# A decoder trunk in split fp32: another order of gates, VectorE's y work spread out, and adding transfers ordered behind GpSimd's powers

## The chip, the cores and the metric

The kernel runs on one core of a Trainium2 chip. The metric is the device time of one execution in microseconds (us), as the median of several runs. TensorE (PE) multiplies, VectorE (DVE) and ScalarE (ACT) work on tiles, GpSimd (POOL) does a few small steps and issues transfers, SyncE (SP) issues most transfers.

## The reference

512 tokens of 1024 features pass one layer; 16 learned meta tokens stand ahead of them and are dropped at the end. All is fp32.

```python
h = concat([pad, meta, x])
h = h + 0.5 * swiglu(rms_norm(h, ffn1_norm), ffn1_w_in, ffn1_w_out)
h = h + token_mixer(rms_norm(h, mix_norm), ...)
h = h + 0.5 * swiglu(rms_norm(h, ffn2_norm), ffn2_w_in, ffn2_w_out)

# rms_norm(x, g) = x * rsqrt(mean(x * x) + EPS) * g
# swiglu(h, w_in, w_out): gate, up = split(h @ w_in); (silu(gate) * up) @ w_out   (2816 hidden units)
# token_mixer: proj = h @ w_in, split into q, k, v of both branches and ga, gb (1024 each)
#   o_fox = attention with a forget gate; o_swa = sliding-window attention with sinks
#   y = sigmoid(ga) * (o_fox @ w_branch_fox) + sigmoid(gb) * (o_swa @ w_branch_swa)
#   return y @ w_out
```

## The kernel before

**Products.** Every fp32 factor is split into a hi part and a lo part: ScalarE casts the hi part (L133), VectorE subtracts it from the value (L140, or L142 with a scale). A product is then three matmuls per 128 rows: weight hi by data hi (L293), weight hi by data lo (L294), weight lo by data hi (L296). In names, `wh`/`wl` are the parts of a weight piece, `xH`/`xL` of the normalised tokens, `yH`/`yL` of `y`, `oW`/`oLs` of an attention output.

**Sevens.** Most large products are done two weight blocks at a time with seven products instead of eight (`seven`, L504), over halves of the tokens and of the inner dimension. The weights of such a unit are loaded as pieces A to D: A is the first blocks and a sum, loaded plainly (SP's queue, `land`, L206) and with an accumulating transfer on GpSimd's queue (`add`, L210) that adds the second block in DRAM to what landed; B, C and D come from `rawC` (also with an add) and `rawD`; VectorE makes B's sums `tc` of both (L232, L233), just before they are cast to `wh` and subtracted to `wl`. The data side needs sums too: S1 to S4, each a pair of hi and lo parts. The first two units of each feed-forward are plain products (gate and up, both token halves).

**Stages**, by the names of the trace: entry, up to 31 us, where token blocks are loaded, their mean squares made, raised to the power -1/2 on GpSimd (`rsq`, L337), scaled (`entry_scale`, L641) and transposed by TensorE (`to_features`, L649); FFN1 to about 375; the mixer's projections and both attentions to about 608; the gates to 700; the output projection to 747; FFN2 to the end.

**The entry.** Blocks 0 to 2 (272 tokens with the meta tokens) go first, blocks 3 and 4 (256 tokens) in `enter_rest` and `enter_second`: one step on VectorE makes both mean squares into `rin`, GpSimd raises both, VectorE scales `xt3` and `xt4`, TensorE transposes each in eight steps.

**The gates.** The first four column blocks (NG = 4) of the fox gate are plain products. For the rest the table `GATES` (L41) gives the order of sevens: (b, m) is column blocks m and m + 1 of the gate of branch b (0 is fox, 1 is sliding). A fox gate multiplies `zA`, which holds the fox branch's output, by its sigmoids. A sliding gate with m below 6 multiplies `oA`, the sliding branch's output, by its sigmoids (`sg`), adds `zA` and makes `yH` and `yL` (`y_out`); with m = 6 it keeps its sigmoids for the two products marked "sliding", which finish `y` (`last_y`). The output projection then goes over two token halves `hf` with eight column blocks `mi` each, and reads all of `y` of its token half; `add_out` adds it to the residual `h2T` and sums squares. Its second half is followed by the power for FFN2 in two parts, r2 (`second_rms`).

**What sets the order.** The code states work in an order, and a scheduler puts each engine's instructions in a row by that order and by hints (`issue_after`, here `after`). Each engine then takes its row strictly in order and waits at semaphores. Loads are stated five pieces ahead of use (`load_to`); `holds` stops them at certain pieces until `release()` is called: after the second rms of the entry, after the attention's buffers are freed, and in FFN2 after the second power.

Of the kernel before, what the change touches and what calls it, by code (L numbers as in the profile page):

```python
# [11 lines left out]
F32 = mybir.dt.float32  # L12
# [8 lines left out]
P = 128  # L21
D = 1024
KD = D // P
S = 512
# [15 lines left out]

GATES = [(1, 0), (1, 2), (0, 4), (1, 4), (0, 6), (1, 6), ("sliding", 6), ("sliding", 7)]  # L41
TH = T // 2
# [40 lines left out]
def kernel(  # L83
# [46 lines left out]
    def hi(o, i, scale=None):  # L130

        if scale is None:
            return A.copy(o, i)  # L133
        return A.activation(o, i, AF.Identity, scale=scale)
# [74 lines left out]
    def add(tile_, ap):  # L209
        G.dma_start(tile_[:, : 128 * ap.shape[1]].rearrange("p (k c) -> p k c", c=128), ap, accum_op=ALU.add)  # L210

# [47 lines left out]
    def release():  # L259
        del holds[0]  # L260

    def split_to(n):
# [73 lines left out]
    def rsq(o, i):  # L336
        G.tensor_tensor(out=o, in0=i, in1=nhalf[: i.shape[0], : i.shape[1]], op=ALU.pow)  # L337

# [1224 lines left out]


    for k in range(0, KD, 4):
        A.dma_start(xg[:, k : k + 4], h1d[:, k : k + 4])
# [29 lines left out]
    xq = lambda tok, feat: xg[:, 4 * feat : 4 * feat + 4, halves[tok]]  # L1596

    at = [spare[:, 2 * i : 2 * i + 2].rearrange("p a (b c) -> p (a b) c", c=HF) for i in (0, 1, 2, 0)]

    def sum_of(i, a, b, op=ALU.subtract):  # L1600
        V.tensor_tensor(out=at[i], in0=a, in1=b, op=op)

    def parts_of(i, name):
        hi(xS[name][:, 0], at[i])
        lo(xS[name][:, 1], at[i], xS[name][:, 0])

    with after(*shared["split"]):
        sum_of(0, xq(0, 0), xq(1, 0))
    parts_of(0, "S3")
# [20 lines left out]
    def y_out(m, c, s):  # L1630
        tt(s, s, zA[:, m, c], ALU.add)
        hi(yH[:, m, c], s)
        lo(yL[:, m, c], s, yH[:, m, c])

    def last_y(m):
        def use(ps):
            s = swa_out(m)
            tt(s, s, ps)
            y_out(m, slice(0, S), s)

        return use
# [54 lines left out]
    h2T = kp.tile([P, KD, S], F32, tag="z", name="h2T")  # L1696
    x2 = kp.tile([P, KD, S], F32, tag="o", name="x2")
    for k in (slice(0, 2), slice(2, KD)):
# [26 lines left out]

    X2 = Halves(None, x2, S // 2)
    for hf in range(2):
        c = slice(S // 2 * hf, S // 2 * (hf + 1))
        for mi in range(KD):
            run(feat_steps(piece, yH, yL, KD, S // 2 * hf, add_out(mi, c), w=S // 2))  # L1730
            if hf and mi == 0:
# [143 lines left out]
```

## Time and profile before

| | us |
|---|---|
| median of 3 runs | 1092.93 (1091.42 to 1093.97) |
| profiled execution, its own time | 1091.91 |
| its span, first to last instruction | 1090.1 |
| PE busy, 8587 instructions | 1072.3 (98%) |
| DVE busy | 891.5 (82%) |
| ACT busy | 656.3 (60%) |
| POOL busy | 194.2 (18%) |

The granted clock of TensorE is 0.998 over the span. A row of the timeline gives the start in us, the duration, engine, line, operation, output and inputs, and in brackets how long the engine was idle before and what ended that. Instructions of one engine overlap: matmuls are pipelined, so a matmul of 0.28 us is followed by the next after about 0.12 us.

### The profile page before, as it was taken

The page shows a single profiled execution, that of the slowest core. Times are in us where ns is not written, and L with a number is a line of the kernel's source. Part 1 is how long each engine was busy: PE and PEld are TensorE (multiplying, and loading weights), DVE is VectorE, ACT ScalarE, POOL GpSimd, SP SyncE. Part 2 cuts the span into 40 slices and gives each one's busy share as a digit, 9 for nine tenths or more (in the row PEclk, how much of TensorE's full clock was granted, in tenths as well). Part 3 has the DMA queues.
Part 4 walks back from the last instruction along what each step waited for, and adds up shares of the span by engine and source line. Part 5 has one row for each costly group of instructions (what it writes and reads, how often), then busy time and mean ns, then how long its engine had stood idle before and what let it go on. Part 6 is the DMA issues. An engine that isn't in the chain of part 4 may idle for free.

```text
span 1090.1 us, 22316 instructions
## 1 busy us (share of the span) xinstructions
PE 1072.3 (98%) x8587; PEld 1038.8 (95%) x8587; DVE 891.5 (82%) x1712; ACT 656.3 (60%) x1241; POOL 194.2 (18%) x229
## 2 busy tenths in 40 slices
PE   7999999999999999999999999999999999999998
PEld 6999999999999999999987799999999999999998
DVE  5978878888889677778897699878998778887895
ACT  5676546646666455456667866545676466645664
POOL 2011111121114430222200110001122211221120
PEclk9999999999999999999999999999999999999999
DMA  8586777678776423112211764467588877886753
GB/s 287 146 221 170 174 193 199 160 197 231 169 191 162 129 77 120 58 60 60 80 59 59 229 166 128 143 224 212 143 207 176 203 189 178 182 195 182 168 119 105
DMA packets 111723, 173.06 MB, mean 159 GB/s; under 512 B 10800, under 2 KB 58160, under 8 KB 111232
## 3 DMA queue, kind: packets, MB, share of 16 engines
q1 hardware_dynamic: 74032, 122.03, 34.6%
q0 software_dynamic: 28768, 37.83, 21.8%
q10 hardware_dynamic: 8816, 11.77, 3.4%
q8 instruction: 67, 1.10, 0.4%
q14 instruction: 40, 0.33, 0.1%
HBM read 167.37 MB, written 6.32 MB: 159 GB/s over the span
## 4 chain that ended last, share of the span: by engine, by line
PE 56%; DVE 6%; ACT 2%; DMA 1%; issue 1%; POOL 0%; ACTq 0%; DVEq 0%; POOLq 0%
PE ps L293 9%; PE ps L296 8%; PE ps L294 8%; PE pt L293 8%; PE pt L294 8%; PE pt L296 8%; DVE wl L140 2%; ACT wh L133 1%; DMA rawC<-in_wg_dram 1%; ACT t L1159 1%; DVE oA L1629 1%; PE pt L1199 1%; PE pt L1244 1%; PE ps L1366 0%; DMA raw<-in_wout_dram 0%
## 5 line engine op out<-in xcount | busy, mean ns | idle before, releaser
L293 PE MATMUL ps<-x,wh 128*128 128x256 f32 (+2 forms) x768 | 219.6, 286 | 1.1 <-ACT pt L514 1.0
L294 PE MATMUL ps<-x,wh 128*128 128x256 f32 (+2 forms) x768 | 219.0, 285 | 0.5 <-DVE x L142 0.4
L296 PE MATMUL ps<-x,wl 128*128 128x256 f32 (+2 forms) x768 | 218.9, 285 | 0.0
L140 DVE TENSOR_TENSOR wl<-raw,wh 128x1024 fp32r<-128x1024 f32 (+3 forms) x125 | 150.2, 1202 | 46.8 <-ACT wh L133 45.2
L133 ACT CAST wh<-raw 128x1024 fp32r<-128x1024 f32 (+3 forms) x125 | 128.4, 1029 | 90.2 <-PE ps L294 56.6
L293 PEld LDWEIGHTS ps<-x,wh 128*128 128x128 f32 x768 | 144.7, 189 | 2.6 <-ACT pt L514 1.2
L294 PEld LDWEIGHTS ps<-x,wh 128*128 128x128 f32 x768 | 144.5, 188 | 1.5 <-DVE x L142 0.9
L296 PEld LDWEIGHTS ps<-x,wl 128*128 128x128 f32 x768 | 144.6, 188 | 0.9
L293 PE MATMUL pt<-x,wh 128*128 128x256 f32 (+2 forms) x424 | 125.4, 296 | 0.2 <-ACT wh L133 0.2
L296 PE MATMUL pt<-x,wl 128*128 128x256 f32 (+2 forms) x424 | 124.5, 294 | 0.0
L294 PE MATMUL pt<-x,wh 128*128 128x256 f32 (+2 forms) x392 | 112.6, 287 | 0.0
L140 DVE TENSOR_TENSOR wl<-tc,wh 128x1024 fp32r<-128x1024 f32 (+1 forms) x70 | 83.5, 1193 | 32.9 <-ACT wh L133 32.6
L133 ACT CAST wh<-tc 128x1024 fp32r<-128x1024 f32 (+1 forms) x70 | 71.8, 1026 | 59.2 <-DVE tc L233 51.3
L293 PE MATMUL ps<-acts,wh 128*128 128x264 f32 (+1 forms) x352 | 100.5, 285 | 0.3 <-ACT pt L514 0.2
L296 PE MATMUL ps<-acts,wl 128*128 128x264 f32 (+1 forms) x352 | 99.8, 284 | 0.0
L294 PE MATMUL ps<-acts,wh 128*128 128x264 f32 (+1 forms) x352 | 99.5, 283 | 0.0
L140 DVE TENSOR_TENSOR wl<-rawC,wh 128x1024 fp32r<-128x1024 f32 (+1 forms) x70 | 84.1, 1202 | 6.1 <-ACT wh L133 5.8
L133 ACT CAST wh<-rawC 128x1024 fp32r<-128x1024 f32 (+1 forms) x70 | 71.6, 1023 | 22.5 <-PE pt L294 16.1
L293 PEld LDWEIGHTS pt<-x,wh 128*128 128x128 f32 x424 | 80.0, 189 | 2.6 <-ACT wh L133 0.4
L296 PEld LDWEIGHTS pt<-x,wl 128*128 128x128 f32 x424 | 79.7, 188 | 2.1
L294 PEld LDWEIGHTS pt<-x,wh 128*128 128x128 f32 x392 | 73.7, 188 | 0.6
L293 PEld LDWEIGHTS ps<-acts,wh 128*128 128x128 f32 x352 | 66.5, 189 | 0.9 <-ACT pt L514 0.4
(417 smaller groups left out, 3249.7 us busy)
## 6 DMA issues: line engine op xcount, KB each, us to landing
rawC<-in_w1i_dram SPq DMA_DIRECT2D x20, 512.0 KB, 4.3
raw<-in_w1i_dram SPq DMA_DIRECT2D x40, 256.0 KB, 4.0
raw<-in_w2i_dram SPq DMA_DIRECT2D x40, 256.0 KB, 3.5
rawC<-in_w2i_dram SPq DMA_DIRECT2D x20, 512.0 KB, 4.4
raw<-in_wm_dram SPq DMA_DIRECT2D x18, 512.0 KB, 4.3
raw<-in_wout_dram SPq DMA_DIRECT2D x16, 512.0 KB, 4.1
rawD<-in_w1i_dram SPq DMA_DIRECT2D x20, 256.0 KB, 4.2
rawC<-in_w1i_dram POOLq DMA_DIRECT2D x20, 256.0 KB, 5.8
```

The lines of the kernel that those rows point to most:

```text
L133: return A.copy(o, i)
L140: return V.tensor_tensor(out=o, in0=i, in1=h, op=ALU.subtract)
L293: PE.matmul(ps, sH, mH, start=first, stop=False, **more)
L294: PE.matmul(ps, sH, mL, start=False, stop=False, **more)
L296: shared["mm"] = PE.matmul(ps, sL, mH, start=False, stop=last, **more)
L1159: shared["exp"] = A.activation(t, t, AF.Exp, bias=nmx, scale=-1.0, accum_out=l[:, j : j + 1])
L1199: PE.matmul(ps[:, :w], q[qx][hb, hp, P * i : P * i + P], k[kx][hb, hp, c0 : c0 + w], start=qx + kx == 0, stop=qx == 1 and not last,)
L1244: PE.transpose(ps[:, c : c + P], ts_[hh][(c // P) % 2][:, c0 : c0 + P], ident)
L1629: tt = lambda o, a, b, op=ALU.mult: V.tensor_tensor(out=o, in0=a, in1=b, op=op)
```

## The change

1. `GATES` has another order: (0, 4), (1, 0), (0, 6), (1, 2), (1, 4), (1, 6).
2. `rsq` notes its instruction; `release()` keeps the last one noted as `held`, and every `add` issued from then on is ordered behind it on GpSimd.
3. The data sum S3 is no longer one subtraction of two blocks of the scaled `xg`, but the sum of two differences, of `xH` and of `xL` (five steps of VectorE), stated ahead of the loads of `xg`.
4. The hi and lo parts of `y` for the second token half are not made with `y`, but in the output projection, two before each of the first four column blocks of the first token half (`later`); the last `y` is split into two halves for that.
5. `x2` takes its buffer at the start of the output projection's second half.

GpSimd, entry (`rin` are the mean squares; the 128x2 steps are the powers of two blocks, `raw` and `rawC` the adding loads). Before:

```order
L337 TENSOR_TENSOR rin<-rin,nhalf 128x2
L940 AFFINE_SELECT cmask<-cmask 128x128
L337 TENSOR_TENSOR rin<-rin,nhalf 128x1
L210 DMA rawC_271<-in_w1i_dram 128x512
L210 DMA rawC_612<-in_w1i_dram 128x512
L210 DMA raw_267<-in_w1i_dram 128x512
L337 TENSOR_TENSOR rin<-rin,nhalf 128x2
L210 DMA raw_575<-in_w1i_dram 128x512
```

After:

```order
L339 TENSOR_TENSOR rin<-rin,nhalf 128x2
L942 AFFINE_SELECT cmask<-cmask 128x128
L339 TENSOR_TENSOR rin<-rin,nhalf 128x1
L339 TENSOR_TENSOR rin<-rin,nhalf 128x2
L211 DMA raw_267<-in_w1i_dram 128x512
L211 DMA rawC_271<-in_w1i_dram 128x512
L211 DMA raw_575<-in_w1i_dram 128x512
L211 DMA rawC_612<-in_w1i_dram 128x512
```

The third power, of blocks 3 and 4, had three adds ahead of it and now has none; the first `rawC` add moved from the first to the second of the adds. At the start of FFN2 the same happens to the last two powers: an add that stood between them now stands behind both.

ScalarE, the first heads and the first seven (`wh_77` is a cast of the first seven's `rawC`, `pt_81` the copy that its next product accumulates on, `x_74` and `acts_61` casts of data parts). Before:

```order
L133 CAST wh_67_469<-tc_66_466 128x1024
L780 DMA acts3_124_864<-in_x_dram 128x1024
L133 CAST x_70_500<-acts_57_421 128x1056
L133 CAST x_74_532<-acts_57_421 128x1056
L133 CAST acts_61_453<-u_40_306 128x528
L133 CAST wh_77_571<-rawC_35_271 128x1024
L514 COPY pt_81_580<-ps_80_579 128x264
L557 COPY p7_83_607<-ps_82_594 128x264
```

After:

```order
L133 CAST wh_67_469<-tc_66_466 128x1024
L133 CAST x_70_500<-acts_57_421 128x1056
L782 DMA acts3_124_864<-in_x_dram 128x1024
L133 CAST wh_77_571<-rawC_35_271 128x1024
L516 COPY pt_81_580<-ps_80_579 128x264
L782 DMA acts3_124_864<-in_x_dram 128x1024
L133 CAST x_74_532<-acts_57_421 128x1056
L133 CAST acts_61_453<-u_40_306 128x528
```

The cast of `wh_77` and the copy moved ahead of the casts of `x_74` and `acts_61`.

VectorE, up to the third gate's sums (`tc_1476`, in both kernels for the third seven of the table; `wh_1477` is the piece made of them). Before:

```order
L1629 TENSOR_TENSOR u2_1468_8639<-u2_1468_8639,rb1_4885 128x256
L1629 TENSOR_TENSOR gz_1472_8665<-pt_1459_8556,rb1_4885 128x256
L1629 TENSOR_TENSOR c22_1474_8685<-pt_1467_8625,p7_1461_8583 128x256
L1629 TENSOR_TENSOR oA_4878<-oA_4878,sg_1469_8643 128x256
L1629 TENSOR_TENSOR oA_4878<-oA_4878,sg_1473_8667 128x256
L1629 TENSOR_TENSOR oA_4878<-oA_4878,zA_4879 128x256 x2
L1629 TENSOR_TENSOR c22_1474_8685<-c22_1474_8685,rb1_4885 128x256
L140 TENSOR_TENSOR yL_8409<-oA_4878,yH_8408 128x256 x2
L1629 TENSOR_TENSOR oA_4878<-oA_4878,sg_1475_8688 128x256
L232 TENSOR_TENSOR tc_1476_8694<-rawC_1465_8608,rawD_1466_8609 128x512
L1629 TENSOR_TENSOR oA_4878<-oA_4878,zA_4879 128x256
L233 TENSOR_TENSOR tc_1476_8694<-tc_1476_8694,rawC_1465_8608 128x512
```

After:

```order
L140 TENSOR_TENSOR wl_1456_8543<-rawC_1441_8455,wh_1455_8542 128x1024
L140 TENSOR_TENSOR wl_1471_8640<-raw_1457_8546,wh_1470_8639 128x1024
L1636 TENSOR_TENSOR gz_1462_8592<-pt_1443_8472,rb1_4885 128x256
L140 TENSOR_TENSOR wD_1464_8597<-rawD_1442_8456,wD_1464_8597 128x512
L1636 TENSOR_TENSOR zA_4879<-zA_4879,sg_1463_8594 128x256
L233 TENSOR_TENSOR tc_1476_8682<-rawC_1465_8600,rawD_1466_8601 128x512
L1636 TENSOR_TENSOR u2_1468_8631<-ps_1460_8565,u2_1468_8631 128x256
L234 TENSOR_TENSOR tc_1476_8682<-tc_1476_8682,rawC_1465_8600 128x512
L1636 TENSOR_TENSOR u2_1468_8631<-u2_1468_8631,rb1_4885 128x256
L1636 TENSOR_TENSOR gz_1472_8655<-pt_1459_8551,rb1_4885 128x256
L140 TENSOR_TENSOR wl_1478_8686<-tc_1476_8682,wh_1477_8685 128x1024
```

Before, 13 steps of `y` of the first two gates (sums with `zA` and `yL`, three and two of them here) stand ahead of the first row of `tc_1476`; after, none, since the first gate makes no `y` and the second gate's follow behind. On SP's queue the loads keep their order but for a few neighbours.

```diff
@@ -38,7 +38,7 @@
 NC = (2, 2)
 NG = 4
 
-GATES = [(1, 0), (1, 2), (0, 4), (1, 4), (0, 6), (1, 6), ("sliding", 6), ("sliding", 7)]
+GATES = [(0, 4), (1, 0), (0, 6), (1, 2), (1, 4), (1, 6), ("sliding", 6), ("sliding", 7)]
 TH = T // 2
 
 
@@ -207,7 +207,8 @@
         shared["load"] = getattr(i, "ins", i)
 
     def add(tile_, ap):
-        G.dma_start(tile_[:, : 128 * ap.shape[1]].rearrange("p (k c) -> p k c", c=128), ap, accum_op=ALU.add)
+        with after(*shared.get("held", ())):
+            G.dma_start(tile_[:, : 128 * ap.shape[1]].rearrange("p (k c) -> p k c", c=128), ap, accum_op=ALU.add)
 
     def load_first(b1, b2, n):
 
@@ -258,6 +259,7 @@
 
     def release():
         del holds[0]
+        shared["held"] = [shared["pow"]]
 
     def split_to(n):
         while state["split"] < min(n, len(pieces)):
@@ -334,7 +336,7 @@
     gmT, g2T = gT[:, 1], gT[:, 2]
 
     def rsq(o, i):
-        G.tensor_tensor(out=o, in0=i, in1=nhalf[: i.shape[0], : i.shape[1]], op=ALU.pow)
+        shared["pow"] = G.tensor_tensor(out=o, in0=i, in1=nhalf[: i.shape[0], : i.shape[1]], op=ALU.pow)
 
     def tok_cols(i):
         return (0, M) if i == 0 else (M + P * (i - 1), P)
@@ -1562,6 +1564,20 @@
     release()
 
 
+    at = [spare[:, 2 * i : 2 * i + 2].rearrange("p a (b c) -> p (a b) c", c=HF) for i in (0, 1, 2, 0)]
+
+    def parts_of(i, name):
+        hi(xS[name][:, 0], at[i])
+        lo(xS[name][:, 1], at[i], xS[name][:, 0])
+
+
+    for x_, o in ((xH, at[0]), (xL, at[1])):
+        for k in range(2):
+            q = [x_.tiles[k][:, :, M + HF * t : M + HF * t + HF].bitcast(F32) for t in range(2)]
+            V.tensor_tensor(out=o[:, 2 * k : 2 * k + 2], in0=q[0], in1=q[1], op=ALU.subtract)
+    V.tensor_tensor(out=at[0], in0=at[0], in1=at[1], op=ALU.add)
+
+
     for k in range(0, KD, 4):
         A.dma_start(xg[:, k : k + 4], h1d[:, k : k + 4])
 
@@ -1594,18 +1610,9 @@
             A.activation(xg[:, k], xg[:, k], AF.Identity, scale=gmT[:, k : k + 1])
 
     xq = lambda tok, feat: xg[:, 4 * feat : 4 * feat + 4, halves[tok]]
-
-    at = [spare[:, 2 * i : 2 * i + 2].rearrange("p a (b c) -> p (a b) c", c=HF) for i in (0, 1, 2, 0)]
-
     def sum_of(i, a, b, op=ALU.subtract):
         V.tensor_tensor(out=at[i], in0=a, in1=b, op=op)
 
-    def parts_of(i, name):
-        hi(xS[name][:, 0], at[i])
-        lo(xS[name][:, 1], at[i], xS[name][:, 0])
-
-    with after(*shared["split"]):
-        sum_of(0, xq(0, 0), xq(1, 0))
     parts_of(0, "S3")
     sum_of(1, xq(1, 0), xq(1, 1))
     sum_of(2, at[1], xq(0, 0))
@@ -1629,14 +1636,28 @@
     tt = lambda o, a, b, op=ALU.mult: V.tensor_tensor(out=o, in0=a, in1=b, op=op)
     def y_out(m, c, s):
         tt(s, s, zA[:, m, c], ALU.add)
-        hi(yH[:, m, c], s)
-        lo(yL[:, m, c], s, yH[:, m, c])
+        y_parts(m, c, s)
+
+
+    later = []
+
+    def y_parts(m, c, s):
+        def does():
+            hi(yH[:, m, c], s)
+            lo(yL[:, m, c], s, yH[:, m, c])
+
+        if c.start:
+            later.append(does)
+        else:
+            does()
 
     def last_y(m):
         def use(ps):
             s = swa_out(m)
             tt(s, s, ps)
-            y_out(m, slice(0, S), s)
+            tt(s, s, zA[:, m], ALU.add)
+            for c in halves:
+                y_parts(m, c, s[:, c])
 
         return use
 
@@ -1694,7 +1715,6 @@
     banks["turn"] = False
 
     h2T = kp.tile([P, KD, S], F32, tag="z", name="h2T")
-    x2 = kp.tile([P, KD, S], F32, tag="o", name="x2")
     for k in (slice(0, 2), slice(2, KD)):
         G.dma_start(h2T[:, k], h1d[:, k])
     r2 = cp.tile([P, NB], F32, name="r2")
@@ -1723,10 +1743,15 @@
             out=x2[:, k, c], in0=h2T[:, k, c], scalar=g2T[:, k : k + 1], in1=rb1[:, c], op0=ALU.mult, op1=ALU.mult
         )
 
-    X2 = Halves(None, x2, S // 2)
     for hf in range(2):
         c = slice(S // 2 * hf, S // 2 * (hf + 1))
+        if hf:
+            x2 = kp.tile([P, KD, S], F32, tag="o", name="x2")
+            X2 = Halves(None, x2, S // 2)
         for mi in range(KD):
+            if not hf and mi < 4:
+                for _ in range(2):
+                    later.pop(0)()
             run(feat_steps(piece, yH, yL, KD, S // 2 * hf, add_out(mi, c), w=S // 2))
             if hf and mi == 0:
                 spread_first = second_rms(0)
```

## The prediction

> **What bounds the kernel now.** I read the page's shares first, then what TensorE waits for, then the timeline around each of its long waits.
>
> ```profile
> span 1090.1 us, 22316 instructions
> PE 1072.3 (98%) x8587; PEld 1038.8 (95%) x8587; DVE 891.5 (82%) x1712; ACT 656.3 (60%) x1241; POOL 194.2 (18%) x229
> PE pt L649 <- DVE xt L641: 5.0, 4, 4.1
> PE ps L293 <- ACT wh L133: 1.9, 1, 1.9
> PE ps L293 <- ACT pt L514: 1.6, 3, 1.0
> PE ps L354 <- POOL r L337: 0.4, 1, 0.4
> ```
>
> TensorE works in 1072.3 of 1090.1 us, and its work stays the same here, so the change can only win from the 17.8 us that are left, and from stretches in which TensorE runs at a lower clock. In the waits the columns are microseconds in all, how many times, and the longest. Three of the largest lie where the change is made: 4.1 us for the scaled tokens (entry), 1.9 us for one ScalarE cast (gates), 1.0 us for a copy (the first heads).
>
> The 4.1 us begin in GpSimd's queue. Below: VectorE makes the mean squares of two token blocks, GpSimd raises them to a power, VectorE scales the blocks, TensorE transposes them.
>
> ```profile
> 19.46 0.17 DVE L631 TENSOR_SCALAR rin<-rin 128x2 f32<-128x2 f32 x1 [0.77 <-ACT sq L616]
> 22.63 0.84 POOL L210 DMA_DIRECT2D raw<-in_w1i_dram  x1 [2.77 <-issue]
> 23.19 1.02 POOL L337 TENSOR_TENSOR rin<-rin,nhalf 128x2 f32<-128x2 f32 x1
> 24.25 1.44 DVE L641 TENSOR_SCALAR xt<-xt,rin 128x1024 f32<-128x1024 f32 x2 [4.07 <-POOL rin L337]
> 20.80 0.28 PE L293 MATMUL ps<-x,wh 128*128 128x264 f32 x1
> 25.15 0.45 PE L649 MATMUL pt<-ident,xt 128*128 128x128 f32 x1 [4.06 <-DVE xt L641]
> 28.35 0.27 PE L649 MATMUL ps<-ident,xt 128*128 128x128 f32 x1
> 26.00:27.00 1.00, 1.00 (x7) 1.00 (x6) 0.37 (x2) 0.00 (x0) 0.00 (x0) 0.50 0.60 84
> ```
>
> The squares are ready at 19.63, but the power starts at 23.19: the adding load of `raw` issued at 22.63 stands ahead of it. TensorE has nothing from 21.08 to 25.15. And it pays twice. The last row is a stretch of 1 us: its length, then busy time and instructions of PE, PEld, DVE, ACT and POOL, the granted clock, the DMA share and GB/s. The clock is at 0.50, so that the 16 transposes from 25.15 to 28.35 stand 0.213 us apart.
>
> **The change part by part.**
>
> *Adds behind the powers.* GpSimd's order shows the power two rows ahead of the place it had, with no add between the powers. What is left of the delay, by the first blocks of the same kernel, where no add is in the way:
>
> ```profile
> 6.27 0.72 POOL L337 TENSOR_TENSOR rin<-rin,nhalf 128x2 f32<-128x2 f32 x1 [4.86 <-DVE rin L631]
> 7.03 0.78 DVE L641 TENSOR_SCALAR xt<-xt,rin 128x1024 f32<-128x1024 f32 x1 [0.71 <-POOL rin L337]
> 8.13 0.27 PE L649 MATMUL pt<-ident,xt 128*128 128x128 f32 x1
> 8.24 0.27 PE L649 MATMUL ps<-ident,xt 128*128 128x128 f32 x1
> ```
>
> The power would start some 0.1 us after 19.63 and take 0.72 (1.02 as it took above): done at 20.45 to 20.75. The first scaling then ends at 21.2 to 21.55, and TensorE starts some 0.17 us later (before: 24.25 plus half of 1.44 is 24.97, and TensorE at 25.15), at 21.4 to 21.7. That is 3.45 to 3.75 us earlier; I take 3.6. Its idle time shrinks to 0.3 to 0.6 us. After 1.90 us of idle time (the gates, below) the clock stayed at 1.00 in the same trace, so I let it stay at 1.00 here; the 15 steps between transposes then go at 0.11 instead of 0.213 us: 1.55 us.
>
> Clock and queue together bring TensorE's first sevens forward by about 5.1 us. VectorE's chain moves by less: 3.6 us at its scalings, and perhaps 4.5 us where its next waits on transposes fall away. It has little to spare there, so up to 0.6 us comes back as small waits on it. The adds themselves wait for the last power now; behind the first of them GpSimd has only other adds, whose readers are VectorE's `tc` sums and `raw` parts of the sevens (a rival below).
>
> *The copy in the first heads.* ScalarE's order also changes: the copy that TensorE waits for stands ahead of a cast that used to come first.
>
> ```profile
> 47.90 1.04 ACT L133 CAST wh<-rawC 128x1024 fp32r<-128x1024 f32 x1
> 48.85 0.37 ACT L514 COPY pt<-ps 128x264 f32<-128x264 f32 x1
> 40.00:50.00 10.00, 9.04 (x75) 8.83 (x74) 10.00 (x14) 6.37 (x10) 1.71 (x2) 1.00 0.77 194
> ```
>
> TensorE is idle 0.96 of the 10 us (9.04 busy). The cast of `wh_77` still stands ahead of the copy; what leaves is the casts of `x_74` and `acts_61`, so wh_77 and the copy both start earlier by about a cast (1.04, the row above). I take the whole 1.0 as won, 0 as the lower bound. With 3.6 and 1.55 and less the 0.6 that comes back: **entry 5.55 us**, from 3.4 (no gain from the copy, the power at its slow end, another 1.0 us lost to VectorE) to 6.3.
>
> *Gates by seven.* A gate of the fox branch (0, m) multiplies `zA` by its sigmoid. A gate of the sliding branch (1, m) with m up to 4 multiplies `oA`, adds `zA` and makes the hi and lo parts of `y`: 8 more steps of VectorE. The order before starts with two of them.
>
> ```profile
> 640.40:650.30 9.90, 9.90 (x86) 9.90 (x85) 9.90 (x23) 6.87 (x15) 2.57 (x3) 1.00 0.63 156
> 650.30:661.60 11.30, 9.19 (x75) 8.77 (x74) 11.21 (x23) 7.57 (x16) 0.86 (x1) 1.00 0.64 160
> 652.62 0.76 DVE L140 TENSOR_TENSOR yL<-oA,yH 128x256 fp32r<-128x256 f32 x2
> 653.64 0.68 DVE L232 TENSOR_TENSOR tc<-rawC,rawD 128x512 f32<-128x512 f32 x1
> 655.52 1.04 ACT L133 CAST wh<-tc 128x1024 fp32r<-128x1024 f32 x1
> 654.43 0.28 PE L296 MATMUL pt<-S,wD 128*128 128x256 f32 x1
> 656.61 0.39 PE L293 MATMUL ps<-S,wh 128*128 128x256 f32 x1 [1.90 <-ACT wh L133]
> 657.57 0.39 PE L293 MATMUL pt<-x,wh 128*128 128x256 f32 x1 [0.21 <-ACT wh L133]
> ```
>
> In both stretches VectorE has next to no gap. After two gates of this kind it makes the third gate's sums (`tc`) so late that TensorE stands 1.90 us and then 0.21: in the second stretch 9.19 of 11.30 is busy, 2.1 idle. With the two slow products behind the waits (0.39 each instead of 0.28) it is 2.3. In VectorE's order 13 steps of `y` (7 additions of `zA`, 6 lo parts) stand ahead of that `tc`; after, none do. At 0.38 us each (0.76 for two) that is 4.9 us, against 2.3 to be gained: enough, with 2.6 to spare. Later only (1,2) and (1,4) stand side by side. Each puts VectorE about 1.1 us behind (2.1 us after two), and now loses two lo steps to the output projection, 0.76: 0.35 behind, 0.7 for both. So I take **2.3 us**, all of it; the low end is 0 (the wait moves to a later gate).
>
> *The lo and hi parts moved to the output projection.* Eight pieces of each go to the first four products of its first token half:
>
> ```profile
> 700.00:711.80 11.80, 11.80 (x99) 11.60 (x98) 6.64 (x9) 4.39 (x6) 1.09 (x2) 1.00 0.69 262
> ```
>
> VectorE is busy 6.64 of 11.80 us there and ScalarE 4.39. Eight steps by 0.38 are 3.0 us on each: 9.7 and 7.4. TensorE has no gap, so this costs **0**, and 3.0 us at most if that cover were gone.
>
> *S3 from xH and xL.* Four subtractions and one addition take the place of one subtraction, and run earlier:
>
> ```profile
> 619.75 1.23 DVE L1601 TENSOR_TENSOR spare<-xg 128x1024 f32<-128x1024 f32 x1 [1.36 <-ACT xg L1594]
> ```
>
> VectorE was idle for 1.36 us ahead of the one that leaves, so its removal gives TensorE nothing; the five that come take about 4 x 0.68 and 1.23, 4 us. They write `spare`, so they wait until the attention has left that buffer, and the parts of `oLs` that feed the next sliding products are queued behind them on VectorE. I take **0**; a loss of up to 1.2 us (one such step in the way) is the bound, and no gain. The later allocation of `x2` issues nothing and counts 0.
>
> *FFN2's start.* The second power used to stand behind an add:
>
> ```profile
> 750.59 0.91 POOL L210 DMA_DIRECT2D raw<-in_w2i_dram  x1 [22.82 <-DVE r L961]
> 751.22 1.02 POOL L337 TENSOR_TENSOR r<-r,nhalf 128x2 f32<-128x2 f32 x1
> 752.30 0.71 PE L354 MATMUL ps<-ident,r 128*128 128x128 f32 x4 [0.42 <-POOL r L337]
> ```
>
> The power would start at about 750.7 instead of 751.22, and TensorE's 0.42 us is gone: **0.4 us**.
>
> **Sum:** 5.55 + 2.3 + 0.4 = 8.25 us. The profiled execution took 1091.91 us, 1.8 more than its span of 1090.1, so the change would take 1083.7 in an execution like it. The median of the runs, 1092.93, stands 1.0 above it: **1084.7 us**.
>
> **The rivals.**
>
> *The clock halves all the same* (6%). Before the transposes TensorE would still stand 0.3 to 0.6 us, and short waits on their scalings can follow. For it: one gap sufficed there. Against it: that gap was 4.06 us, while 1.90 us idle at 654.7 left 1.00 in the stretch around it. It would cost the 1.55 us: 1086.2. [...]
>
> *The gates gain nothing* (10%): VectorE, full in both stretches above, is late for a later gate's cast instead, and 2.3 us go back: 1087.0. For it: (1,2) and (1,4) now follow each other. Against it stand the 2.6 us to spare.
>
> *The entry gains nothing* (5%): something else holds the second blocks, such as their own scaling or a bank of PSUM. 5.55 us go back: 1090.2. The order of GpSimd speaks against it.
>
> *Slower: the adding loads land late* (5%). All four first adds now leave GpSimd after 20.75 us, one after the other. The first `rawC` was issued at 15.79, and is now second in the line.
>
> ```profile
> 15.79 1.05 POOL L210 DMA_DIRECT2D rawC<-in_w1i_dram  x1 [6.26 <-DMA rawC<-in_w1i_dram]
> rawC<-in_w1i_dram POOLq DMA_DIRECT2D x20, 256.0 KB, 5.8
> 41.22 0.68 DVE L232 TENSOR_TENSOR tc<-rawC,rawD 128x512 f32<-128x512 f32 x1
> 30.00:40.00 10.00, 10.00 (x80) 9.51 (x79) 9.56 (x15) 6.23 (x12) 0.00 (x0) 1.00 0.27 86
> 642.44 0.86 POOL L210 DMA_DIRECT2D raw<-in_wg_dram  x1 [0.43 <-DVE c L1629]
> 642.10 1.22 DVE L140 TENSOR_TENSOR wl<-tc,wh 128x1024 fp32r<-128x1024 f32 x1
> ```
>
> Issued at about 22.5 it lands at 28.3 (5.8 us), or at 34.1 if one add waits for the other; it is read at 41.22, now some 4.5 earlier, 36.7. Beyond that every microsecond late stops TensorE, and a stop of some 4 us may halve the clock again, as the one at the entry did. To eat the gain of 8.25 it would have to land after 45 us; that takes both adds in series, each at twice the 5.8 (22.5 + 23.2 = 45.7), because the plain loads of the same stage crowd them out. With the clock halved again this gives 1092.9 - 8.25 + 9.0 + 1.55 = 1095.2. Against it: the DMA share was 0.27 from 30 to 40 us.
>
> [...]
>
> **How the numbers follow.** The forecast has 74%. Its time is 1084.7, and the best ends of its terms, 6.3 + 2.3 + 0.4 = 9.0, give 1083.9; VectorE's new free time may also end some of the many small waits, so the range reaches down to 1081.3. Upward, the forecast with the low end of the entry and 1.2 us lost at S3 gives 1084.7 + 2.15 + 1.2 = 1088.05, and with no gain at the gates 1090.3; the range ends at 1089.5, which holds the first two rivals. About 0.2%, 2.2 us, is what a measurement of this kernel can tell from no change. Faster by more: the forecast, the clock, the gates and half of the third, less what I can't see: 0.88. Within: half of the third and a part of the fourth, 0.07. Slower: 0.05.
>
> **What would show it.** Right: the power of the second blocks ends ahead of 21 us and no add stands ahead of it; TensorE's transposes stand 0.11 apart with a clock of 1.00 from 21 to 25; no wait on `wh` near 655; products of FFN2 without 0.42 us. Wrong: an idle TensorE from 30 to 50 us on `tc` or `rawC` (adds late); a wait of over 1 us in the fifth or sixth gate; VectorE without a gap from 700 to 712 and TensorE waiting there.

## The result and the profile after

The changed kernel takes 1082.19 us (median of 5 runs, 1081.80 to 1083.46), the kernel before on the same chip 1092.57 (1090.32 to 1093.97). The ratio is 0.9911, 95% interval 0.9896 to 0.9926. Forecast was 1084.7 against 1092.93, a ratio of 0.9925.

The page of the changed kernel and what TensorE waits for (in all, times, longest):

```profile
span 1080.4 us, 22336 instructions
PE 1070.7 (99%) x8587; PEld 1038.4 (96%) x8587; DVE 892.1 (83%) x1718; ACT 656.6 (61%) x1243; POOL 194.0 (18%) x229
PE pt L651 <- DVE xt L643: 0.6, 1, 0.6
PE ps L295 <- ACT pt L516: 0.6, 2, 0.4
```

TensorE has the same 8587 matmuls, so the k-th of them can be compared in two traces: how much earlier it starts at a landmark is what was won up to there. Below, this is worked out for the changed kernel and for six of the experiments that follow, against the kernel before, in us and by stage (minus is won). Inside the gates the order of the products differs between the kernels, so there it is the ends of the stages that compare:

| kernel | start, to 20 us | entry, to 31 | first heads and seven, to 57 | to 584 | gates, to 705 | output projection, to 741 | FFN2's start, to 754 | to the end | sum |
|---|---|---|---|---|---|---|---|---|---|
| changed kernel | +0.24 | -4.68 | -0.87 | -0.30 | -3.15 | -0.30 | -0.68 | -0.04 | -9.78 |
| held_only | -0.05 | -4.69 | -0.88 | -0.19 | +1.80 | -0.22 | -0.68 | 0 | -4.91 |
| gates_only | -0.44 | -0.95 | +0.01 | -0.26 | -0.64 | +0.16 | +0.20 | 0 | -1.92 |
| defer_only | -0.13 | -1.84 | 0 | -0.44 | -1.02 | -0.23 | +0.39 | -0.01 | -3.28 |
| gates_defer | +0.13 | -1.11 | 0 | -0.37 | -3.11 | -0.03 | +0.09 | 0 | -4.39 |
| no_defer | +0.02 | -4.68 | -0.88 | -0.36 | -0.68 | -0.21 | -0.68 | +0.01 | -7.46 |
| s3_only | -0.07 | -1.36 | -0.01 | -0.23 | +1.25 | -0.02 | +0.34 | +0.02 | -0.08 |

The entry, in the timeline of the changed kernel: mean squares, power, first add, scaling, the last product before, the first and the last transpose.

```profile
19.70 0.17 DVE L633 TENSOR_SCALAR rin<-rin 128x2 f32<-128x2 f32 x1 [0.77 <-ACT sq L618]
19.95 0.71 POOL L339 TENSOR_TENSOR rin<-rin,nhalf 128x2 f32<-128x2 f32 x1 [10.53 <-DVE rin L633]
21.47 1.05 POOL L211 DMA_DIRECT2D raw<-in_w1i_dram  x1 [0.81 <-DMA raw<-in_w1i_dram]
20.69 1.42 DVE L643 TENSOR_SCALAR xt<-xt,rin 128x1024 f32<-128x1024 f32 x2 [0.82 <-POOL rin L339]
20.68 0.28 PE L295 MATMUL ps<-x,wh 128*128 128x264 f32 x1
21.59 0.30 PE L651 MATMUL pt<-ident,xt 128*128 128x128 f32 x1 [0.63 <-DVE xt L643]
23.55 0.27 PE L651 MATMUL ps<-ident,xt 128*128 128x128 f32 x1
22.00:23.00 1.00, 1.00 (x11) 0.84 (x8) 0.92 (x4) 0.36 (x1) 1.00 (x3) 1.00 0.00 0
```

The power follows the squares, the adds stand behind it, and TensorE waits 0.63 us instead of 4.06: 3.43 us won. The clock in the last row is 1.00, and the 16 transposes take 1.96 us from first to last start instead of 3.20: another 1.24. This execution had lost 0.24 us at the start, where the matmuls ahead of the first transpose stood 0.21 us apart up to 7.62 us instead of 4.42 (0.11 from then on), so that TensorE is 4.4 us ahead at the first sevens.

The copy of the first seven, and what is left of its wait:

```profile
42.50 0.36 ACT L516 COPY pt<-ps 128x264 f32<-128x264 f32 x1 [0.54 <-PE ps L298]
46.89 0.39 PE L295 MATMUL ps<-x,wh 128*128 128x264 f32 x1
40.00:50.00 10.00, 9.89 (x81) 9.68 (x80) 9.93 (x14) 6.14 (x11) 0.39 (x1) 1.00 0.87 264
```

ScalarE now waits for TensorE's product and not the other way round. A smaller wait of 0.11 us is new at 46.89; with the slow starts around it it costs 0.37. The gates, with the third gate's sums:

```profile
641.32 0.69 DVE L233 TENSOR_TENSOR tc<-rawC,rawD 128x512 f32<-128x512 f32 x1
644.32 1.23 DVE L140 TENSOR_TENSOR wl<-tc,wh 128x1024 fp32r<-128x1024 f32 x1 [0.44 <-ACT wh L133]
644.80:654.60 9.80, 9.80 (x85) 9.80 (x84) 9.80 (x22) 6.64 (x15) 1.72 (x2) 1.00 0.75 186
664.40:674.20 9.80, 9.80 (x85) 9.79 (x84) 9.80 (x20) 6.71 (x16) 0.00 (x0) 1.00 0.37 90
```

The `tc` sums begin at 641.32 instead of 653.64: 12.3 us earlier, of which 5.6 come from the stages before. VectorE is still full in the gates, but TensorE doesn't wait at all from 630 to 695 us. The parts of `y` that were to move:

```profile
689.42 1.44 DVE L140 TENSOR_TENSOR yL<-oA,yH 128x256 fp32r<-128x256 f32 x4
694.18 0.75 DVE L140 TENSOR_TENSOR yL<-oA,yH 128x256 fp32r<-128x256 f32 x2
691.20:703.00 11.80, 11.80 (x98) 11.56 (x97) 6.70 (x10) 4.49 (x7) 1.09 (x2) 1.00 0.69 259
```

All sixteen lo parts of `y` are done by 695, and only two of them stand in the output projection, which starts at 691.4. The others that were to move stand beside the last gate and the two sliding products, where VectorE has some idle time (busy 9.95 of 10.90 us from 684.1 to 695). At FFN2's start the power comes first:

```profile
741.58 0.69 POOL L339 TENSOR_TENSOR r<-r,nhalf 128x2 f32<-128x2 f32 x1 [22.87 <-DVE r L963]
742.33 0.91 POOL L211 DMA_DIRECT2D raw<-in_w2i_dram  x1
742.66 0.61 PE L356 MATMUL ps<-ident,r 128*128 128x128 f32 x4
```

### The profile page after: what moved, and what is told of

Its sections match the earlier page's. It is cut to its first block, busy times and chain, and to the rows that moved or that the text cites. A ratio compares the mean times of both kernels' runs of the same rounds, so it can differ in the third digit from the quotient of the medians.

```text
span 1080.4 us, 22336 instructions
## 1 busy us (share of the span) xinstructions
PE 1070.7 (99%) x8587; PEld 1038.4 (96%) x8587; DVE 892.1 (83%) x1718; ACT 656.6 (61%) x1243; POOL 194.0 (18%) x229
## 4 chain that ended last, share of the span: by engine, by line
PE 90%; DVE 4%; ACT 3%; issue 2%; DMA 0%; POOL 0%; SPq 0%; ACTq 0%; DVEq 0%; POOLq 0%
PE ps L295 15%; PE ps L298 15%; PE ps L296 15%; PE pt L295 13%; PE pt L296 13%; PE pt L298 13%; ACT wh L133 1%; DVE wl L140 1%; ACT t L1161 1%; PE pt L1201 1%; PE pt L1246 1%; DMA xt<-in_x_dram 0%; PE ps L1368 0%; DVE t L1164 0%; PE ps L1201 0%
```

## The experiments

**The adds alone** (held_only): part 2 of the change in the kernel before.

```diff
-        G.dma_start(tile_[...], ap, accum_op=ALU.add)
+        with after(*shared.get("held", ())):
+            G.dma_start(tile_[...], ap, accum_op=ALU.add)
     def release():
         del holds[0]
+        shared["held"] = [shared["pow"]]
```

> The kernel before, with only the adds ordered behind GpSimd's powers. Theory (each term has its own place): TensorE's first transposes of the second blocks at 21.6 us, the entry 5.3 us shorter by the first sevens (3.4 of waiting, 1.6 of clock, 0.9 of the copy, less 0.4 of a new wait and 0.2), 0.3 at the end of FFN1, 0.7 at the start of FFN2, nothing in the gates (the wait of 1.9 us on the cast stays): the time 6.3 us below the kernel before. Rival (the parts need each other: the faster entry comes partly from VectorE's other work): less than 5 us.

Measured: 1086.86 us (6 runs) against 1092.27 (25 runs), ratio 0.9947, interval 0.9931 to 0.9963. By stage the entry (4.69), the copy (0.88), 0.2 at the end of FFN1 and the 0.68 at FFN2 are all there, 6.4 in sum. But its profile shows 1.80 us lost in the gates, which the edit doesn't touch. The wait is the same as in the kernel before; what follows it isn't. Below, the wait and the 3 us behind it in this kernel, then the same 3 us in the kernel before (last three columns: granted clock, DMA share, GB/s):

```profile
650.81 0.39 PE L295 MATMUL ps<-S,wh 128*128 128x256 f32 x1 [1.90 <-ACT wh L133]
652.40:655.40 3.00, 3.00 (x15) 3.00 (x15) 2.56 (x4) 1.38 (x4) 0.00 (x0) 0.50 0.47 156
```

```profile
658.10:661.10 3.00, 3.00 (x27) 3.00 (x27) 3.00 (x6) 1.63 (x4) 0.00 (x0) 1.00 0.79 223
```

The clock halved after 1.90 us of idle time here, and did not in the profile on which the prediction rests; the last section shows what differs. By the starts of the matmuls it costs 1.55 us. Of the six runs of this kernel five have a mean clock of 0.998 and take 1086.56 to 1087.11; the one with 1.000 takes 1085.12. So the theory on the places holds. The medians stand 5.4 apart and not 6.3, which fits a half clock in the gates in most executions; one execution alone was profiled. The rival's "less than 5 us" is met by the span of that execution (4.91), but not for the rival's reason, since the entry won all that was forecast.

**The order of gates alone** (gates_only), and **the moved parts of `y` alone** (defer_only):

```diff
-GATES = [(1, 0), (1, 2), (0, 4), (1, 4), (0, 6), (1, 6), ("sliding", 6), ("sliding", 7)]
+GATES = [(0, 4), (1, 0), (0, 6), (1, 2), (1, 4), (1, 6), ("sliding", 6), ("sliding", 7)]
```

> The kernel before, with only the table of gates in the new order; the hi and lo parts of y stay with their gates. Theory (the order alone takes the 13 steps of y from ahead of the third gate's sums): the wait of 1.9 us on the cast and the two slow starts behind it are gone, 2.7 to 3.1 us less, entry and FFN2 as before. Rival (the moved parts of y are needed too, since two gates with y now follow each other): the wait comes back in the fifth or sixth gate, a gain of under 1 us.

```diff
-        hi(yH[:, m, c], s)
-        lo(yL[:, m, c], s, yH[:, m, c])
+        y_parts(m, c, s)            # kept in `later` if c is the second token half
...
+            if not hf and mi < 4:
+                for _ in range(2):
+                    later.pop(0)()
```

> The kernel before, with only the hi and lo parts of y for the second token half stated in the output projection, in the old order of gates. Of the 13 steps of y, 8 stand ahead of the end of the third gate's sums then, so 5 x 0.34 = 1.7 us are won there at least. Theory (the order does it, the moving is not needed): 1.7 to 2.4 us less, so that either edit alone takes most of the same wait. Rival (the moving does nothing without the order, as VectorE stays full): under 0.5 us less.

Measured: the order alone 1090.22 us, ratio 0.9988 (0.9976 to 0.9999); the moving alone 1089.83, ratio 0.9975 (0.9963 to 0.9987). By stage the gates win 0.64 and 1.02 us. The entry of both profiles is 1 to 2 us shorter than that of the kernel before although nothing was changed there; that belongs to the last section. TensorE's waits in the gates, first of the order alone, then of the moving alone:

```profile
PE ps L293 <- ACT wh L133: 0.7, 1, 0.7
PE ps L296 <- DVE wl L140: 0.5, 1, 0.5
PE pt L293 <- DVE c L1629: 0.4, 1, 0.4
```

```profile
PE pt L293 <- ACT wh L133: 0.5, 2, 0.3
PE ps L296 <- DVE wl L140: 0.2, 1, 0.2
```

With the order alone the wait at the third gate is gone (2.7 us by the starts of the matmuls), and 2.1 us come back at 671 and 684 us, in the fifth and sixth gates. With the moving alone the wait of 1.90 us is gone and three short ones stand in its place. My theory that either edit alone takes most of it fell. The rival of the order's run held; the moving's 1.02 us lies between its theory (1.7 to 2.4) and its rival (under 0.5).

**Both together** (gates_defer):

> The kernel before, with the new order of gates and the moved parts of y. Theory: 3.1 us less in the gates as in the changed kernel, 0.3 more at the first sums of the output projection, so 3.0 to 3.5 us less, and at most 0.5 more than the order alone. Rival (the two edits add up): 4.5 us less.

Measured: 1087.65 us, ratio 0.9951 (0.9935 to 0.9968); by stage 3.11 in the gates, as in the changed kernel, and no wait there. That is more than the sum of the two alone (0.64 + 1.02). The theory held in the size and fell in "at most 0.5 more than the order alone". The medians stand 4.6 us apart and not 3.1. The mean clocks point to a half-clock stretch in the gates that is gone: 19 of the 25 executions of the kernel before have 0.996 or less, and none of the 8 of this one. How much of the 1.5 us is due to it, and how much to a shorter entry, these runs don't separate.

**The changed kernel without the moved parts** (no_defer):

```diff
     def y_out(m, c, s):
         tt(s, s, zA[:, m, c], ALU.add)
-        y_parts(m, c, s)
+        hi(yH[:, m, c], s)
+        lo(yL[:, m, c], s, yH[:, m, c])
```

> The changed kernel without the moved parts of y (hi and lo parts stay with their gates). The order alone gave 2.7 us at the third gate and lost 2.1 us again at 671 and 684 us. Theory (order and moving need each other): the same here, 2.0 to 2.6 us more than the changed kernel, as waits in the fifth and sixth gates. Rival (the shifted start of the gates or the early S3 had already freed VectorE): under 0.7 us more.

Measured: 1084.46 us (1084.25 to 1085.25), 2.3 above the changed kernel; by stage 0.68 won in the gates instead of 3.15. The waits are the same three as with the order alone, 0.7, 0.5 and 0.4 us. The theory held: the order needs the moving.

**S3 alone** (s3_only):

```diff
-    with after(*shared["split"]):
-        sum_of(0, xq(0, 0), xq(1, 0))
+    for x_, o in ((xH, at[0]), (xL, at[1])):
+        for k in range(2):
+            ...  V.tensor_tensor(out=o[:, 2 * k : 2 * k + 2], in0=q[0], in1=q[1], op=ALU.subtract)
+    V.tensor_tensor(out=at[0], in0=at[0], in1=at[1], op=ALU.add)
```

> The kernel before, with only S3 made from xH and xL. Theory (the step that leaves stood in VectorE's idle time, and the five that come fit ahead of the sliding products): within 0.3 us of the kernel before from 600 to 640 us and no other change in the gates; the entry differs from execution to execution by up to 1.6 us in kernels with the old adds and is left out of the comparison. Rival (the five steps are in the way): up to 1.2 us more at 615 us.

Measured: 1091.97 us, ratio 1.0001 (0.9989 to 1.0013). From 584 us to the third gate it stays at the same distance to the kernel before within 0.03 us, so the edit costs and gains nothing there. In its profile the gates lose 1.25 us, again behind the wait of 1.90 us and at a clock of 0.50:

```profile
656.50:659.50 3.00, 3.00 (x15) 3.00 (x15) 2.58 (x4) 1.37 (x4) 0.00 (x0) 0.50 0.66 199
```

**Later adds** (late_adds, late_adds_48, late_adds_72): the changed kernel with GpSimd kept busy between the power and the first add.

```diff
+        for _ in range(16):            # 48, 72
+            with after(shared["pow"]):
+                shared["pow"] = G.tensor_tensor(out=nhalf[:, 6:8], in0=nhalf[:, 4:6], in1=nhalf[:, 4:6], op=ALU.add)
         release()
```

> The changed kernel with sixteen small GpSimd steps between the last power of the entry and the first adding load, so that all four adds start some 11 us later, at 32 to 34 us instead of 21.5 to 23.3; the rows of TensorE, VectorE and ScalarE stay as they are. Theory (the adds have 6 to 9 us of slack, and beyond it each microsecond stops TensorE): a wait of 3 to 6 us between 30 and 45 us, and the time 3 to 7 us above the changed kernel. Rival (the sevens' other loads are the later ones, so the adds have far more slack): under 1 us.

> As before with 48 small GpSimd steps (0.35 us each, as the sixteen took 5.6 us) ahead of the first adding load: the adds start at some 37 us, 15.6 us later than in the changed kernel, and the first lands at some 41.5. TensorE first uses what is made of it at 40.8 us, and the cast and the difference in between take 2.2 us. Theory (slack of about 12 us, then one to one): a wait of 2 to 4 us between 40 and 48 us, the span 2 to 4 us longer. Rival (still hidden): no wait.

> With 72 small steps the adds start at some 45.5 us, 8.4 us later than with 48. Theory (beyond the slack each microsecond late stops TensorE, and a stop of over 3 us can halve its clock): 8 to 11 us more than with 48 steps, so that the span is over 1091 and the changed kernel has lost its gain. Rival (part of the stop is caught up, since other work is moved up behind it): under 6 us more.

The sixteen steps took 5.6 us, not 11, so the adds came only 4.5 us later. 48 steps took 19.6, and with a further idle time of 2.87 us the adds came 21.6 us later; with 72 steps it was 25.1. The last two kernels were executed once each. The first add with 16 steps:

```profile
25.94 1.05 POOL L211 DMA_DIRECT2D raw<-in_w1i_dram  x1 [0.38 <-issue]
```

With 48 steps: the first add, the cast of what it brings, the first matmul that needs it, and two stretches behind.

```profile
43.06 1.05 POOL L211 DMA_DIRECT2D raw<-in_w1i_dram  x1 [2.87 <-issue]
47.51 1.04 ACT L133 CAST wh<-raw 128x1024 fp32r<-128x1024 f32 x1 [15.07 <-issue]
48.60 0.59 PE L295 MATMUL ps<-x,wh 128*128 128x264 f32 x1 [7.67 <-ACT wh L133]
48.00:50.00 2.00, 0.95 (x3) 0.64 (x3) 1.42 (x2) 0.55 (x1) 0.00 (x0) 0.50 1.09 160
62.00:64.00 2.00, 2.00 (x11) 2.00 (x11) 2.00 (x5) 1.52 (x3) 0.00 (x0) 0.50 0.81 256
```

With 72 steps, the first add and the same matmul; then that matmul in the changed kernel:

```profile
46.61 1.05 POOL L211 DMA_DIRECT2D raw<-in_w1i_dram  x1 [0.37 <-issue]
52.02 0.59 PE L295 MATMUL ps<-x,wh 128*128 128x264 f32 x1 [11.65 <-ACT wh L133]
```

```profile
40.78 0.28 PE L295 MATMUL ps<-x,wh 128*128 128x264 f32 x1
```

At 4.5 us later nothing is lost: 4.67 and 0.87 us stay won by 57 us, and the time is 1082.58. (Its profile stands 1.8 us worse in the output projection, where ScalarE waited 5.90 us for a weight load of `wout` in that execution; its median doesn't.) At 21.6 us later ScalarE waits 15.07 us for the first add, and TensorE 7.67. The clock is at a half (0.50) from 45.1 to 55.4 us and again from 58.8 to 65.6. From 31 to 57 us 15.96 are lost instead of 0.87 won, and the kernel takes 1099.1 us, 7 more than before. At 25.1 us later it is 18.75 and 1101.34.

The slack can be worked out from these rows. Where TensorE waits for the add, the matmul starts 5.54 us behind it with 48 steps and 5.41 with 72; in the changed kernel it starts 19.31 behind it. So the adds have some 13.8 us of slack: more than the 6 to 9 of the first run's theory, which a delay of 4.5 us couldn't test, and close to the 12 of the second. Beyond it the stop grows about one to one: the adds came 3.55 us later with 72 steps than with 48, the matmul 3.42. The rival of the last run, "under 6 us more", came true because the adds were 3.55 and not 8.4 us later; up to this matmul no other work makes up for the stop. By 57 us some 1.2 of these 3.42 us are gone, counted like the rows from the start of the span. Behind this matmul the clock stood at a half for 10.7 us with 72 steps and for 13.6 with 48, which would account for about that much.

**The rest of the entry's wait** (split_rms, half_scale, split_half):

```diff
-        inline(("V", lambda: entry_rms(3, 5)), ("V", lambda: entry_scale(3, "V")), ("V", lambda: entry_scale(4, "V")))
+        # split_rms
+        inline(("V", lambda: entry_rms(3, 4)), ("V", lambda: entry_rms(4, 5)))
+        inline(("V", lambda: entry_scale(3, "V")), ("V", lambda: entry_scale(4, "V")))
+        # half_scale: entry_rms(3, 5), entry_scale(3) in columns 0 to 512 and 512 to D, entry_scale(4)
+        # split_half: entry_rms(3, 4), entry_scale(3, 0 to 512), entry_rms(4, 5), entry_scale(3, 512 to D), entry_scale(4)
```

> The changed kernel with the mean squares of the two second blocks made and raised apart, so that the first power needn't wait for the second block's squares (ready 1.0 us after the first's). Theory (the rest of the wait at 20.7 us is that chain): the wait of 0.63 us falls under 0.2 and the entry is 0.5 to 0.8 us shorter; the time 0.5 to 0.8 us below the changed kernel. Rival (VectorE or the second block is then the one waited for): the 0.6 us come back within the transposes or at the next wait on VectorE, no gain.

> The changed kernel with the third block scaled in two halves of 512 features, so that TensorE's first four transposes need only the first half; the copy of the first seven keeps its place ahead of the casts. Theory (the rest of the wait at 20.7 us is power and scaling): 0.3 to 0.4 us less waiting there and the rest unchanged, 0.3 us below the changed kernel, too little for the measured time to show and only visible in the stretch. Rival (VectorE's own pace is the bound): none.

> The changed kernel with the squares of the two second blocks raised apart and the third block scaled in two halves, in an order in which the copy of the first seven stays ahead of the casts (with the split alone it fell behind them, which cost 1.0 us). Theory: the wait at 20.7 us goes, the copy's gain stays, 0.5 to 0.9 us below the changed kernel. Rival: the fourth block becomes the late one, and its wait of 0.5 us, seen with the split alone, stays: under 0.3 us.

Measured: 1082.77, 1082.73 and 1083.06 us, against 1082.19 of the changed kernel; none beats it. With the power split, the third block is there in time and the wait goes to the fourth (first row, split_rms, 0.35 us; third, split_half, 0.57). Without the split, TensorE waits as before (last row, half_scale). And the split alone put the copy of the first seven behind the casts again, as in the kernel before (second row):

```profile
21.66 0.33 PE L651 MATMUL pt<-ident,xt 128*128 128x128 f32 x1 [0.35 <-DVE xt L643]
44.35 0.40 PE L295 MATMUL ps<-x,wh 128*128 128x264 f32 x1 [0.86 <-ACT pt L516]
21.83 0.33 PE L651 MATMUL pt<-ident,xt 128*128 128x128 f32 x1 [0.57 <-DVE xt L643]
21.59 0.30 PE L651 MATMUL pt<-ident,xt 128*128 128x128 f32 x1 [0.61 <-DVE xt L643]
```

By stage the entry wins 4.93, 4.65 and 4.74 us, against 4.68. The rivals held: what is waited for is the fourth block's chain or the same power. The second row shows besides that the 0.9 us of the copy come from where the scheduler puts it, and that an edit of the entry can move it.

## Why the prediction was right, and where not

- **Adds behind the powers.** Forecast: TensorE at 21.4 to 21.7, clock at 1.00, entry shorter by 5.1 (3.6 of waiting, 1.55 of clock), of which up to 0.6 comes back. Measured: 21.59, 1.00, and 4.7 up to the first sevens (3.43 and 1.24; the transposes took 1.96 us and not 1.65). Right in mechanism and size; held_only shows it alone.
- **The copy.** 1.0 forecast as the whole wait; 1.24 won and 0.37 given back at 46.89. What I had charged with 0.6 as waits on VectorE came as 0.31 within the transposes and 0.37 at a copy. Entry and copy together: 5.55 forecast, 4.68 + 0.87 = 5.55 measured. That the two agree to the last digit is luck, since the terms under it were off by up to 0.3.
- **Gates.** The cause was right: the steps of `y` ahead of the third gate's sums (twelve stand ahead of the first row of `tc`, the thirteenth between its two rows). The size was too small, 2.3 for 3.15. At the third gate it is 2.7: across a wait the next matmul starts 0.28 us plus the idle time behind the last one instead of 0.12, and the one after it 0.22 behind that, so that each of the two waits costs 0.26 more than its idle time and not 0.11. In the kernel before these are the starts at 654.43 and 656.61, which the prediction shows, and the one that follows:

```profile
656.83 0.29 PE L294 MATMUL ps<-S,wh 128*128 128x256 f32 x1
```

Another 0.5 us were won at 687 us, which I left out. And the order does not do it alone, as I had argued with "2.6 us to spare": that held for the third gate. Without the moving 2.1 us come back in the fifth and sixth gates, which is what I had counted for two gates side by side (1.1 us each) before I took off 0.76 for the moved parts. I called "the gates gain nothing" a rival of 10%; for the order alone it would have been the likeliest.
- **The moved parts.** I put eight lo parts into the output projection and found room there. Two came there; the scheduler placed the rest beside the sliding products, where VectorE had some idle time. The cost of 0 was right for another reason than the room that I had found, and the order of the changed kernel, which I had, shows where they went.
- **S3**: 0 forecast, 0 measured.
- **FFN2's start.** 0.4 forecast, 0.68 measured; left out were the 0.26 us that a wait costs beyond its idle time, as in the gates.
- **Sum.** 8.25 forecast; 9.78 in the spans. The 1.5 us between are 0.85 in the gates and some 0.3 each at the end of FFN1, in the output projection and at FFN2's start, less 0.24 at the very start, where the first matmuls stood 0.21 us apart for longer. The 0.3 at the end of FFN1 and in the output projection have no run of their own, and their cause stays open; both places vary by as much between kernels that don't touch them. The medians stand 10.4 us apart, 0.6 more than the profiled executions. The profiled execution of the kernel before had a mean clock of 0.998, while 42 of 51 others have 0.995 to 0.997; that fits a half-clock stretch that most executions lose in the gates and that the forecast did not count.
- **The clock.** That 1.90 us idle leave the clock at full speed was read from one execution, and is wrong as a rule: behind the same wait the clock was 0.50 in held_only and s3_only. The entry's full clock came out all the same: 1.00 behind 0.63 us idle. The length of a stop alone doesn't tell the clock behind it (3.51 us idle left 1.00, 2.67 left 0.50, at the entry); the last section sets the stops beside the times at which the clock changes.
- **Slower by late adds.** The mechanism exists, and it costs more than I gave: 1095 forecast for a landing at 45.7, 1099.1 for one at some 47.5. For the stop and the clock I had 9.0 + 1.55 = 10.55; measured by 57 us are 15.96 + 0.87 = 16.8. The first stop is 7.8 of it; the rest comes from a clock that was at a half in two stretches, where I had counted one of 16 transposes, and from further waits behind the stop. What is late first is `raw`, whose cast stands ahead of the `tc` sums that I had named.

## What to carry to other kernels

A transfer that waits for something, put ahead of a small step on an in-order queue, makes that step wait for it too (here the power started 3.56 us behind its squares, and 0.08 with the add behind it); order the queue by who is waited for. A wait that one edit removes can come back two stages on where the engine behind it is still full (2.7 us won at the third gate, 2.1 back at the fifth and sixth), so test the edits one by one and together. And read a scheduler's order for where a deferred step really lands. Before the clock behind a wait is read from one profile as a rule, a second execution is worth looking at (behind 1.90 us idle it was 1.00 once and 0.50 twice).

## What the runs showed that I had not expected

*Stops of like length left the clock at a half in some executions and at full speed in others.* Idle time of TensorE at the entry, and whether the clock behind it was halved (0.50) or not (1.00), in six executions: 4.06 us, halved (kernel before); 3.51, not halved (defer_only); 3.34, halved (gates_only); 2.81, halved (gates_defer); 2.67, halved (s3_only); 0.63, not halved (the changed kernel). The two that stand against each other, as the first transpose after the wait and a stretch behind it, defer_only and then s3_only:

```profile
24.46 0.30 PE L649 MATMUL pt<-ident,xt 128*128 128x128 f32 x1 [3.51 <-DVE xt L641]
25.00:26.00 1.00, 1.00 (x10) 0.83 (x8) 1.00 (x3) 0.44 (x2) 0.66 (x1) 1.00 0.34 59
```

```profile
23.69 0.30 PE L649 MATMUL pt<-ident,xt 128*128 128x128 f32 x1 [2.67 <-DVE xt L641]
25.00:26.00 1.00, 1.00 (x8) 0.95 (x6) 1.00 (x4) 1.00 (x4) 0.00 (x0) 0.50 0.91 96
```

The length of the stop doesn't order them. What differs is how the stop lies to the times at which the clock changes. In the trace of the kernel before the clock changes at 4.42, 24.90, 28.31 and 1089.86 us, so 20.48, 3.413 and 1061.55 apart; in that of the changed kernel at 7.62 and 1079.41, 1071.79 apart. These are 6, 1, 311 and 314 times 3.413 us. The half clock behind the stops lasts some 3.4 us in gates_only, gates_defer, s3_only (entry) and held_only (gates), and some 10.2 and 6.8 in each of the two kernels with very late adds.

So I cut the traces into steps of 3.41 us, counted from a change of the clock. In defer_only, whose clock does not change there, the place of the steps is my reckoning: the stop is split between two, with TensorE busy 1.75 and 1.57 us. In s3_only, whose clock halves at 24.80, most of the stop falls into one step, busy 1.11:

```profile
19.21:22.62 3.41, 1.75 (x15) 1.53 (x13) 0.60 (x2) 0.86 (x3) 1.17 (x3) 1.00 1.02 247
22.62:26.03 3.41, 1.57 (x13) 1.40 (x13) 2.46 (x5) 0.47 (x2) 1.60 (x3) 1.00 0.73 125
```

```profile
21.38:24.80 3.42, 1.11 (x10) 1.14 (x11) 2.01 (x4) 0.00 (x1) 2.30 (x3) 1.00 1.04 203
```

The wait of 1.90 us in the gates shows the same. In the kernel before a step ends at 656.37, 184 steps behind 28.31 and inside the wait, and it is busy for 1.76 us; in held_only, whose matmuls stand 0.21 us apart from 652.43 on, the whole wait and the short one behind it lie in one step, busy for 1.31, and the next is at a half:

```profile
652.95:656.37 3.42, 1.76 (x15) 1.56 (x14) 3.42 (x9) 2.32 (x5) 0.86 (x1) 1.00 0.33 96
```

```profile
648.71:652.13 3.42, 1.31 (x9) 0.90 (x7) 3.35 (x7) 3.25 (x6) 0.31 (x1) 1.00 0.52 96
```

In the traces of the kernel before and of the changed kernel the steps at full clock with TensorE busy for 0.00 us (the entry's stop), 0.34 and 0.56 (each the last step of its trace) were followed by half clock, and all others, busy for 1.76 us or more, were not. With the rows above, 1.11 and 1.31 were followed by it, 1.57 and 1.75 were not. That settles no limit: in late_adds_48 the 3.4 us at full clock between two half-clock stretches, busy for 1.05 to 2.45 us by the rows of that profile, were followed by half clock too, and in late_adds_72 those with 1.38 to 1.50. In the gates of held_only one step at half clock cost 1.55 us. In 51 runs of the kernel before beside these experiments, 19 with a mean clock of 0.995 average 1092.9 us and 8 with 0.998 average 1090.5. So a stop cost its own length here, and about 1.5 us more in executions in which half clock followed, and one profile shows one such case.

*The old place of the adds made the time uneven.* The add ahead of the power waits for a plain load; it left at 22.63, 21.47, 21.95 and 21.52 us in the profiles of the kernel before, gates_only, defer_only and gates_defer, in the kernel before 0.52 us after the last landing of that load at 22.11, and the power behind it moved along, 0.56 us later each time. Five runs each of the kernel before and of the changed kernel spread over 3.7 and 1.7 us; the 25 of the kernel before beside held_only spread over 5.8 (1089.39 to 1095.16), and the five of no_defer over 1.0. Some of the larger spread may be the clock, which such stops left at a half in some executions and not in others; these runs don't separate the two.
